# Forming the low halves of the attention weights on GpSimd instead of VectorE, in a two-block transformer kernel

## The chip, the cores and the metric

The kernel runs on one core of a Trainium2 chip. A core has several engines that run side by side, each through its own queue of instructions in a fixed order: TensorE (PE; its weight loads are listed as PEld), VectorE (DVE), ScalarE (ACT), GpSimd (POOL) and SyncE (SP), which here issues the transfers from memory. They wait for each other through semaphores. SBUF is the working memory that all of them reach, PSUM the one into which PE writes its products. The metric is the time of one execution on the device, in microseconds, lower is better; the number compared is the median of several runs.

## The reference

Two transformer blocks, one after the other, on 512 tokens of width 1024, all in float32. The first has a differential attention, a SwiGLU feed-forward part, a sliding-window attention with sinks and a second feed-forward part; the second block has convolution mixers, a convolution feed-forward part, a windowed attention over the tokens and 256 context rows, and a last feed-forward part. The three attentions are the places of this change. Cut to their weights:

```python
# first attention
q, k, v = jnp.split(h @ w_qkv, [DA_QK, 2 * DA_QK], axis=-1)      # 1024 x 3072
...
return o.reshape(B, S, DA_V) @ w_o                                # 1024 x 1024
# second attention
k, v = jnp.split(rms_norm(x, kv_norm) @ w_kv, 2, axis=-1)         # 1024 x 512
q = (h @ w_q).reshape(B, S, SW_KV_HEADS, SW_GROUP, HEAD_DIM)      # 1024 x 1024
...
return o.reshape(B, S, SW_HEADS * HEAD_DIM) @ w_o
# third attention
q, k, v = jnp.split(h @ w_qkv, [Q_W, Q_W + KV_W], axis=-1)        # 1024 x 1536
...
y = jnp.moveaxis(out, 0, 1).reshape(bsz, length, Q_W) @ w_o
```

## The kernel before, in words

Every float32 matrix that goes into a product is split in two halves of PE's float32r format: `hi` is the value rounded to float32r (a cast, by ACT or by DVE), and `lo` is what the rounding left, `src - hi` (a subtraction, by DVE). A product is then three matmuls, hi x hi, hi x lo and lo x hi, added up in PSUM (`mm3`).

Weights are loaded by `wload`: a transfer of 128 partitions x 1024 columns (512 KB; 768 columns for some) into one of two raw buffers, then `split` into one of three slots of a `hi` and a `lo` tile. A raw buffer is free for the next transfer when its subtraction is done, a slot when PE has read it for the last time. With `gain=` (the key, value and query weights of the second attention) another path is taken that multiplies by a norm's gain. The first two weights of the first attention are loaded with `urgent=0`, before everything else.

The three attentions are `diff_attn` and two calls of `gqa` (`cfg` 1 and 2). Each interleaves projections of the next heads with the softmax of the current ones (`weave`). In `gqa`, POOL copies one column for each head and block (`nc.gpsimd.tensor_copy(e[:, n:n+1], ns)`), the sink's logit, which ACT's exponential reads together with the scores. Between the attentions stand the feed-forward parts and the mixers, where POOL has 120 additions of 128x256 for a convolution.

The order of the instructions is not that of the code. `Rec` collects all operations with their dependences; `issue` orders them by a list schedule: `forward` starts on each engine the ready operation of highest priority, with each operation's duration from `cost`, and `backward` sets the priorities; the seven rounds of it serve the whole program. Casts are `flex`: `forward` may put them on ACT or on DVE, whichever is planned to be free. So every change of an engine or of a cost can reorder all engines' queues, and the order is fixed when the program is built. Line 390 of the profile is the place where an ordered operation is issued, so all rows carry that line, and rows are told apart by engine, operation, tiles and size: `arenaF` holds float32 tiles, `arenaR` float32r tiles, `arenaZ` either, `psum_t` is PSUM. A weight's low half is the row TENSOR_TENSOR arenaR<-arenaF,arenaR of 128x1024 or 128x768.

Of the kernel before, what the change touches and what calls it, by code (L numbers as in the profile page):

```python
# [9 lines left out]
F32 = mybir.dt.float32  # L10
# [4 lines left out]
ALU = mybir.AluOpType  # L15
# [183 lines left out]
class _Eng:  # L199
    def __init__(self, rec, name):  # L200
        self._r, self._n = rec, name
# [5 lines left out]
class Rec:  # L207
# [112 lines left out]
    def cost(self, eng, fn, a, k, outs, ins):  # L320
        o = outs[0]
        n = self.fsize(o)
        ps = any(x.tensor.name == self.pname for x in ins)
        if eng == "tensor":
            dt = (k.get("rhs") if fn == "matmul" else a[1]).dtype
            if fn == "transpose":
                return 59 if dt == F32R else 109
            if dt == F32:
                return max(n * 1.685, 214)
            if dt == F32R:  # L330
                return max(n * 0.4222, 107)
            return max(n * 0.4222, 29)
        if eng == "scalar":
            return n / 1.2 + (51 if ps else 93) + (93 if len(ins) > 1 else 0) + (93 if len(outs) > 1 else 0)
        if eng == "sync":
            b = 4
            for _, c in o.ap:
                b *= c
            return b
        if fn in ("tensor_tensor_reduce", "scalar_tensor_tensor") and isinstance(k["scalar"], bass.AP):  # L340
            return (n + 124) / 0.96
        if fn == "reduce_sum":
            n = self.fsize(ins[0])
        if eng == "gpsimd":
            return 2.1 * n + 148 if fn == "tensor_tensor" else 80 + n
        one = fn in ("tensor_copy", "tensor_scalar", "memset", "tensor_scalar_mul") and not ps
        return ((n / 2 if one and n > 64 else n) + 65) / 0.96

# [168 lines left out]
class Ker:  # L517
    def __init__(self, tc, a, es, start, stop):
        self.tc, self.a, self.start, self.stop = tc, a, start, stop
        real = tc.nc  # L520
        cp = es.enter_context(tc.tile_pool(name="arena", bufs=1))
        pp = es.enter_context(tc.tile_pool(name="banks", bufs=1, space=PSUM))
        self.psum = pp.tile([P, 8 * 512], F32, name="psum_t")[:]
        self.rec = self.nc = Rec(real, self.psum)
        self.bg = iter(())
        self.wslot = 0
        self.cls = {}
        self.size = {"R": R_SIZE, "F": F_SIZE, "Z": Z_SIZE}
        self.ar = {}
        for n, dt in (("R", F32R), ("F", F32)):  # L530
            self.ar[n] = cp.tile([P, self.size[n]], dt, name=f"arena{n}")[:]
            self.rec.rows[self.ar[n].tensor.name] = (n, self.size[n])
        self.zpool = None
        self.zmode = None
        self.nz = 0
        self.top = {"R": 0, "F": 0}
        self.flip = False
        self.psets = {}
        self.segment("R")
# [64 lines left out]
                              **{q: w for q, w in zip(names[1:], shape[1:])})  # L604
        return ap

    def phase(self, psets, keep=(), wslots=3):


        self.wslots = wslots  # L610
        self.wslot %= 3
        keep = dict(zip("RF", keep))
        if not keep:
            self.flip = not self.flip
        self.lo, self.hi = dict(self.top), {m: self.size[m] for m in "RF"}
        for m, w in keep.items():
            if self.flip:
                self.hi[m] -= w
            else:
                self.lo[m] += w  # L620
        self.zlo = 0
        self.cls = {k: v for k, v in self.cls.items() if k[0] not in ("ph", "z")}
        self.psets = {k: [v, 0] for k, v in psets.items()}
# [37 lines left out]
        o, w = _ROWS[name]  # L661
        return self.rowt[:, o:o + w] if o < NROW1 else self.rowd[:, o - NROW1:o - NROW1 + w]

    def split(self, src, hi, lo, scale=None):

        self.copy(hi, src)
        self.nc.vector.tensor_tensor(out=lo, in0=src, in1=hi.bitcast(F32), op=ALU.subtract)

    def rsqrt(self, v, n, y, ln=None):

# [36 lines left out]
    def wload(self, src, n=1024, gain=None, urgent=1000000, parts=1):  # L707

        nc = self.nc
        raw = self.t("wp", [1024], "wraw", bufs=2)[:, :n]  # L710
        j = self.wslot
        self.wslot = (j + 1) % self.wslots
        pool = "wp" if j < 3 else "ph"
        hi, lo = (self.t(pool, [1024], f"w{x}{j}", F32R)[:, :n] for x in ("hi", "lo"))
        rec = self.rec
        b, rec.bias = rec.bias, -urgent
        if gain is None:
            for x in range(parts):
                sl = slice(x * n // parts, (x + 1) * n // parts)
                self.dma(raw[:, sl], src[:, sl])  # L720
                self.split(raw[:, sl], hi[:, sl], lo[:, sl])
        else:
            self.dma(raw, src)
            k = n // len(gain)
            for j, g in enumerate(gain):
                sl = slice(j * k, (j + 1) * k)
                nc.scalar.activation(hi[:, sl], raw[:, sl], AF.Copy, scale=g)
                nc.vector.scalar_tensor_tensor(out=lo[:, sl], in0=raw[:, sl], scalar=g, in1=hi[:, sl].bitcast(F32),
                                               op0=ALU.mult, op1=ALU.subtract)
        rec.bias = b  # L730
        return hi, lo
# [621 lines left out]
    def diff_attn(self, X):  # L1353
        nc, a = self.nc, self.a
        if True:
            ph = None
            self.phase({"g": [0, 1], "r": [2], "s": [3, 4], "t": [5, 6], "o": [7], "f": [2, 3, 4, 7]})
            X.x = [None] * KT
            X.h = [None] * KT
            w0 = []  # L1360
# [32 lines left out]
            o, res, v = {}, {}, {}  # L1393
# [53 lines left out]
            for h in range(8):  # L1447
                fill = []
                if h < 7:
                    r = qks[h + 1][1]  # L1450
# [275 lines left out]
    def gqa(self, X, C, cfg):  # L1726
# [4 lines left out]
        if True:  # L1731
            ph = None
            if b2:
# [1 line left out]
                at = self.cls["ph", "t2l"][1] - 512  # L1735
                spare = {("ph", w): ["R", at + x, 1024, 1, 0] for w, x in (("whi3", 0), ("wlo3", 1024))}
            self.phase({"g": [0, 1], "s": [2, 3], "n": [4], "t": [5, 6], "o": [7]} if b2 else
                       {"g": [0, 1], "r": [2], "s": [3, 4], "t": [5, 6], "o": [7]})
            if b2:
                tab = (self.t("ph", [4, 1, 64], "axC"), self.t("ph", [4, 1, 64], "axS"), 1)  # L1740
                ax = a["axial"].rearrange("p (s a o d) -> p s a o d", s=2, a=4, o=1)
# [62 lines left out]
            o = {}  # L1804
# [25 lines left out]
            r, p = qs[0][1], qs[1][0]  # L1830
            for x in (r, r, p, r, r, p):
                next(x)
            for g in range(4):
                fill = []
                if g < 3:
                    r = qs[g + 1][1]
# [459 lines left out]
```

## Time and profile before

| | |
|---|---|
| runs, device time | 2524.76, 2527.75, 2531.60 us; median 2527.75 |
| the profiled execution | 2529.82 us, its span on the core 2528.0 us, mean granted PE clock 0.997 |
| busy in the span | PE 2493.7, PEld 2312.1, DVE 2198.9, ACT 1446.9, POOL 133.0 us |
| first attention | to about 252 us |
| second attention | about 603 to 800 us; its softmax part from 690 |
| third attention | about 1900 to 2145 us |

The span is what the profiler saw from the first to the last instruction. Busy times are unions of records; a matmul's end is modelled, so PE can be short of its peak where it is shown busy. Positions in the rows are us from the start of the span. Every duration used is of this one execution.

### The profile page before, as it was taken

How to read it: one execution, taken by the hardware profiler on the slowest of the kernel's cores; microseconds unless marked ns; L12 is line 12 of the kernel's file. 1: busy time of each engine (PE TensorE's matmuls, PEld its weight loads, DVE VectorE, ACT ScalarE, POOL GpSimd, SP SyncE). 2: the span in 40 equal slices, each digit the busy share in tenths (PEclk: the TensorE clock that was granted, in tenths of full speed). 3: DMA queues.
4: the chain of work that ended last, by engine and by line, in shares of the span. 5: the costliest groups of instructions: out<-in, count | busy, mean ns of one | idle time of the engine just before them, and what ended most of it. 6: DMA issues, size and time to landing. Idle time of an engine off the chain costs nothing.

```text
span 2528.0 us, 42483 instructions
## 1 busy us (share of the span) xinstructions
PE 2493.7 (99%) x16346; PEld 2312.1 (91%) x16346; DVE 2198.9 (87%) x4210; ACT 1446.9 (57%) x2795; POOL 133.0 (5%) x252
## 2 busy tenths in 40 slices
PE   8999999999999999999999999999999999999998
PEld 8998988888988989999889999999999988999897
DVE  8887999996699989888986998888887899998886
ACT  6877622223798545456664844434456798555464
POOL 0000000000010000003650000000000000000000
PEclk9999999999999999999999999999999999999999
DMA  4111566662213354432121121222221101323322
GB/s 146 62 55 65 188 204 221 211 214 89 76 37 123 125 185 144 168 131 84 51 76 59 43 76 59 75 67 76 68 70 56 43 26 51 109 84 100 115 75 89
DMA packets 73068, 252.52 MB, mean 100 GB/s; under 512 B 8480, under 2 KB 10656, under 8 KB 72608
## 3 DMA queue, kind: packets, MB, share of 16 engines
q1 hardware_dynamic: 72864, 249.80, 29.0%
q8 instruction: 128, 2.10, 0.3%
q14 instruction: 76, 0.62, 0.1%
HBM read 247.67 MB, written 2.10 MB: 99 GB/s over the span
## 4 chain that ended last, share of the span: by engine, by line
PE 92%; DVE 3%; POOL 2%; ACT 2%; issue 1%; DMA 0%; SPq 0%; DVEq 0%; POOLq 0%; ACTq 0%
PE psum_t L390 92%; POOL arenaZ L390 2%; DVE arenaF L390 2%; DVE arenaR L390 1%; ACT arenaR L390 1%; ACT arenaF L390 1%; DMA arenaF<-in_wqkv_dram 0%; SPq L390 0%; ACT L390 0%; ACT arenaZ L390 0%; ACT L388 0%; DVEq L2292 0%; POOLq L390 0%; ACT psum_t L390 0%; DVE psum_t L390 0%
## 5 line engine op out<-in xcount | busy, mean ns | idle before, releaser
L390 PE MATMUL psum_t<-arenaR 128*128 128x256 f32 (+3 forms) x13220 | 2156.4, 316 | 16.5 <-ACT arenaR L390 8.1
L390 PEld LDWEIGHTS psum_t<-arenaR 128*128 128x128 f32 (+1 forms) x13220 | 1917.4, 189 | 151.9 <-ACT arenaR L390 11.0
L390 ACT CAST arenaR<-arenaF 128x1024 fp32r<-128x1024 f32 (+5 forms) x622 | 537.8, 874 | 612.4 <-PE psum_t L390 397.4
L390 DVE TENSOR_TENSOR arenaR<-arenaF,arenaR 128x1024 fp32r<-128x1024 f32 (+5 forms) x586 | 599.7, 1033 | 73.0 <-ACT arenaR L390 64.6
L390 ACT ACTIVATE arenaF<-arenaF 128x256 f32<-128x256 f32 (+10 forms) x946 | 498.4, 552 | 171.7 <-DVE arenaF L390 138.5
L390 PE MATMUL psum_t<-arenaZ,arenaR 128*128 128x256 f32 (+3 forms) x2112 | 452.5, 326 | 1.4 <-ACT arenaZ L390 0.9
L390 DVE TENSOR_TENSOR arenaF<-arenaF 128x512 f32<-128x512 f32 (+7 forms) x715 | 404.4, 582 | 26.6 <-ACT arenaF L390 22.3
L390 PEld LDWEIGHTS psum_t<-arenaZ,arenaR 128*128 128x128 f32 x2112 | 335.2, 188 | 34.1 <-DVE arenaF L390 1.7
L390 DVE TENSOR_TENSOR arenaF<-psum_t,arenaF 128x256 f32<-128x256 f32 (+2 forms) x420 | 196.6, 482 | 80.8 <-PE psum_t L390 79.6
L390 DVE SCALAR_TENSOR_TENSOR arenaF<-arenaF 128x511 f32<-128x511 f32 (+9 forms) x555 | 244.0, 473 | 6.9 <-ACT arenaF L390 5.4
L390 DVE CUSTOM_DVE_ANT_0 arenaF<-arenaF 128x1024 f32<-128x1024 f32 x160 | 204.7, 1279 | 8.3 <-DMA arenaF<-in_wmod_dram 4.6
L390 DVE SCALAR_TENSOR_TENSOR arenaF<-psum_t,arenaF 128x256 f32<-128x256 f32 (+3 forms) x293 | 167.1, 595 | 35.5 <-PE psum_t L390 34.5
L390 ACT COPY arenaF<-psum_t 128x256 f32<-128x256 f32 (+2 forms) x285 | 106.7, 389 | 143.0 <-PE psum_t L390 133.3
L390 ACT CAST arenaR<-psum_t 128x512 fp32r<-128x512 f32 (+4 forms) x333 | 156.9, 480 | 31.3 <-PE psum_t L390 28.1
L390 POOL TENSOR_TENSOR arenaZ<-arenaZ,arenaF 128x256 f32<-128x256 f32 x120 | 103.1, 861 | 428.9 <-ACT arenaF L390 420.0
L390 PE MATMUL psum_t<-arenaF 128*128 128x128 f32 (+2 forms) x730 | 112.6, 268 | 7.4 <-DVE arenaF L390 3.2
L390 DVE CUSTOM_DVE_ANT_0 arenaF<-psum_t,arenaF 128x256 f32<-128x256 f32 (+3 forms) x208 | 103.6, 510 | 13.4 <-PE psum_t L390 11.5
L390 POOL COPY arenaF<-arenaF 128x1 f32<-128x1 f32 x128 | 29.7, 256 | 1565.6 <-issue 637.8
L390 DVE TENSOR_TENSOR arenaR<-psum_t,arenaR 128x512 fp32r<-128x512 f32 (+4 forms) x169 | 98.0, 589 | 14.8 <-ACT arenaR L390 13.3
L390 PEld LDWEIGHTS psum_t<-arenaF 128*128 128x128 f32 x730 | 89.3, 153 | 19.0 <-DVE arenaF L390 3.8
L390 ACT ACTIVATE arenaR<-arenaF 128x256 fp32r<-128x256 f32 (+1 forms) x152 | 72.1, 513 | 26.8 <-DVE arenaF L390 16.8
L390 DVE SCALAR_TENSOR_TENSOR psum_t<-arenaF,psum_t 128x512 f32<-128x512 f32 x120 | 81.8, 745 | 1.6 <-ACT psum_t L390 1.5
(53 smaller groups left out, 618.0 us busy)
## 6 DMA issues: line engine op xcount, KB each, us to landing
arenaF<-in_wmod_dram SPq DMA_DIRECT2D x96, 512.0 KB, 3.9
arenaF<-in_wgu_dram SPq DMA_DIRECT2D x88, 512.0 KB, 3.6
arenaF<-in_wup_dram SPq DMA_DIRECT2D x88, 512.0 KB, 3.2
arenaF<-in_wqkv_dram SPq DMA_DIRECT2D x35, 512.0 KB, 3.2
arenaF<-in_wdn_dram SPq DMA_DIRECT2D x30, 512.0 KB, 4.1
arenaF<-in_wd_dram SPq DMA_DIRECT2D x32, 448.0 KB, 3.7
arenaF<-in_wab_dram SPq DMA_DIRECT2D x20, 512.0 KB, 3.2
arenaF<-in_wd_dram SPq DMA_DIRECT2D x16, 512.0 KB, 3.3
```

Source lines behind the costliest of these rows:

```text
L390: getattr(getattr(self.nc, e), fn)(*a, **k)
```

## The change

`split` gets a switch that puts the subtraction on POOL, `wload` throws it in the phases that are opened with `lowpool=True` (the three attentions) unless the load has `urgent=0` or a gain, and `cost` gets another price for a POOL operation on two tensors of 512 columns or more. Sixty subtractions move: 32 in the first attention (8 of 768 columns), 8 in the second, 20 in the third.

```diff
-            return 2.1 * n + 148 if fn == "tensor_tensor" else 80 + n
+            return (2.1 * n + 148 if n < 512 else 3.36 * n) if fn == "tensor_tensor" else 80 + n
...
-    def phase(self, psets, keep=(), wslots=3):
+    def phase(self, psets, keep=(), wslots=3, lowpool=False):
...
         self.wslots = wslots
+        self.lowpool = lowpool
...
-    def split(self, src, hi, lo, scale=None):
+    def split(self, src, hi, lo, pool=False):
 
         self.copy(hi, src)
-        self.nc.vector.tensor_tensor(out=lo, in0=src, in1=hi.bitcast(F32), op=ALU.subtract)
+        eng = self.nc.gpsimd if pool else self.nc.vector
+        eng.tensor_tensor(out=lo, in0=src, in1=hi.bitcast(F32), op=ALU.subtract)
...
-                self.split(raw[:, sl], hi[:, sl], lo[:, sl])
+                self.split(raw[:, sl], hi[:, sl], lo[:, sl], self.lowpool and urgent)
...
-            self.phase({"g": [0, 1], "r": [2], "s": [3, 4], "t": [5, 6], "o": [7], "f": [2, 3, 4, 7]})
+            self.phase({"g": [0, 1], "r": [2], "s": [3, 4], "t": [5, 6], "o": [7], "f": [2, 3, 4, 7]}, lowpool=True)
...
-                       {"g": [0, 1], "r": [2], "s": [3, 4], "t": [5, 6], "o": [7]})
+                       {"g": [0, 1], "r": [2], "s": [3, 4], "t": [5, 6], "o": [7]}, lowpool=True)
```

Three places of the queues follow, as they stand in the two programs. POOL's queue from the mixers to the third attention, where the 128x1024 rows are the subtractions and the 128x1 rows the sink columns:

```order
 L390 TENSOR_TENSOR arenaZ_10453<-arenaZ_10453,arenaF 128x256 x120
-L390 COPY arenaF<-arenaF 128x1 x64
-L2292 UNCONDITIONAL_BRANCH
-L2292 ISA
+L390 TENSOR_TENSOR arenaR<-arenaF,arenaR 128x1024 x4
+L390 COPY arenaF<-arenaF 128x1 x12
+L390 TENSOR_TENSOR arenaR<-arenaF,arenaR 128x1024 x5
+L390 COPY arenaF<-arenaF 128x1 x3
```

The third attention's 64 copies stood together; now its 20 subtractions stand before and between them, the first four ahead of all copies.

DVE's queue about twenty rows into the program, at the start of the first attention, before the change. The 128x1024 row is a weight's low half; the other rows are sums of squares, the input's low halves and small table work:

```order
L390 TENSOR_TENSOR arenaR<-arenaF,arenaR 128x1024
L390 TENSOR_TENSOR arenaF<-arenaF 128x512
L390 SCALAR_TENSOR_TENSOR arenaF<-arenaF 128x128
L390 CAST arenaR<-arenaF 128x128
L390 TENSOR_SCALAR arenaF<-arenaF 128x128
L390 TENSOR_TENSOR arenaF<-arenaF 128x128 x2
L390 TENSOR_REDUCE arenaF<-arenaF 128x2
```

The same place in the changed program:

```order
L390 TENSOR_TENSOR arenaF<-arenaF 128x512
L390 SCALAR_TENSOR_TENSOR arenaF<-arenaF 128x128
L390 TENSOR_TENSOR arenaF<-arenaF 128x128
L390 TENSOR_SCALAR arenaF<-arenaF 128x128
L390 TENSOR_REDUCE arenaF<-arenaF 128x2
```

The low half is gone and the rows behind it have closed up; most of those that are left read two operands from SBUF.

PE's queue from the beginning of the program, before the change (128x256 are projections, the 128x128 rows from `arenaR` transposes of the first head's queries and keys):

```order
L390 MATMUL psum_t<-arenaR 128x256 x122
L390 MATMUL psum_t<-arenaF 128x1 x4
L390 MATMUL psum_t<-arenaR 128x256 x164
L390 MATMUL psum_t<-arenaR 128x128 x4
L390 MATMUL psum_t<-arenaR 128x256 x9
```

And in the changed program:

```order
L390 MATMUL psum_t<-arenaR 128x256 x115
L390 MATMUL psum_t<-arenaF 128x1 x4
L390 MATMUL psum_t<-arenaR 128x256 x123
L390 MATMUL psum_t<-arenaR 128x128 x4
L390 MATMUL psum_t<-arenaR 128x256 x19
```

The first transposes have moved ahead of 48 projections' matmuls.

## Rows read from the trace of the kernel before

**Rows 1.** The page, part 1: busy us, share of the span, instructions.

```profile
PE 2493.7 (99%) x16346; PEld 2312.1 (91%) x16346; DVE 2198.9 (87%) x4210; ACT 1446.9 (57%) x2795; POOL 133.0 (5%) x252
```

**Rows 2.** Busy us by stretch: length, engines (instructions), PE clock, DMA share, GB/s.

```profile
16.00:75.00 59.00, 58.96 (x495) 58.63 (x496) 52.15 (x145) 43.79 (x101) 0.00 (x0) 1.00 0.29 96
75.00:252.00 177.00, 174.54 (x1309) 165.01 (x1307) 149.95 (x416) 133.92 (x330) 0.00 (x0) 0.99 0.18 60
690.00:800.00 110.00, 105.24 (x713) 90.60 (x712) 103.05 (x286) 106.48 (x294) 10.57 (x48) 1.00 0.21 73
1900.00:1925.00 25.00, 21.20 (x157) 19.95 (x156) 21.74 (x56) 16.06 (x36) 0.00 (x0) 0.94 0.29 98
1925.00:2145.00 220.00, 216.09 (x1565) 200.33 (x1565) 192.02 (x466) 184.52 (x372) 13.98 (x64) 0.99 0.11 39
```

**Rows 3.** Groups on DVE, 16:252 (two), 690:800, 1900:2145: count | busy, mean ns | idle before.

```profile
L390 DVE TENSOR_TENSOR arenaR<-arenaF,arenaR 128x1024 fp32r<-128x1024 f32 x24 | 29.3, 1219 | 3.9 <-ACT arenaR L390 3.8
...
L390 DVE TENSOR_TENSOR arenaR<-arenaF,arenaR 128x768 fp32r<-128x768 f32 x8 | 7.6, 955 | 2.3 <-ACT arenaR L390 2.3
...
L390 DVE TENSOR_TENSOR arenaR<-arenaF,arenaR 128x1024 fp32r<-128x1024 f32 x8 | 9.7, 1215 | 0.3 <-ACT arenaR L390 0.3
...
L390 DVE TENSOR_TENSOR arenaR<-arenaF,arenaR 128x1024 fp32r<-128x1024 f32 x20 | 24.4, 1219 | 7.9 <-ACT arenaR L390 7.9
```

**Rows 4.** POOL: a group in 1194.8:1204.5, and the timeline at 685 (start, length).

```profile
L390 POOL TENSOR_TENSOR arenaZ<-arenaZ,arenaF 128x256 f32<-128x256 f32 x12 | 8.9, 739 | 0.9
...
685.32 0.18 POOL L390 COPY arenaF<-arenaF 128x1 f32<-128x1 f32 x1 [106.51 <-ACT arenaF L390]
```

**Rows 5.** Timelines of POOL and of DVE in the mixers, about 1190.4:1195.

```profile
1190.49 5.04 POOL L390 TENSOR_TENSOR arenaZ<-arenaZ,arenaF 128x256 f32<-128x256 f32 x4
...
1190.97 1.34 DVE L390 TENSOR_TENSOR arenaR<-arenaF,arenaR 128x1024 fp32r<-128x1024 f32 x1
1192.23 0.74 DVE L390 SCALAR_TENSOR_TENSOR psum_t<-arenaF,psum_t 128x512 f32<-128x512 f32 x1
1192.89 1.21 DVE L390 TENSOR_TENSOR arenaR<-arenaF,arenaR 128x1024 fp32r<-128x1024 f32 x1
```

**Rows 6.** Timeline of DVE in the first attention, five places.

```profile
19.10 1.22 DVE L390 TENSOR_TENSOR arenaR<-arenaF,arenaR 128x1024 fp32r<-128x1024 f32 x1
20.24 0.68 DVE L390 TENSOR_TENSOR arenaF<-arenaF 128x512 f32<-128x512 f32 x1
...
39.85 1.22 DVE L390 TENSOR_TENSOR arenaR<-arenaF,arenaR 128x1024 fp32r<-128x1024 f32 x1
...
42.51 0.69 DVE L390 TENSOR_TENSOR arenaR<-arenaF,arenaR 128x512 fp32r<-128x512 f32 x1
...
78.57 1.22 DVE L390 TENSOR_TENSOR arenaR<-arenaF,arenaR 128x1024 fp32r<-128x1024 f32 x1
79.71 0.75 DVE L390 SCALAR_TENSOR_TENSOR arenaF<-psum_t,arenaF 128x512 f32<-128x512 f32 x1
80.37 0.55 DVE L390 CUSTOM_DVE_ANT_0 arenaF<-psum_t,arenaF 128x384 f32<-128x384 f32 x1
...
80.84 0.42 DVE L390 TENSOR_TENSOR arenaF<-arenaF 128x256 f32<-128x256 f32 x1
...
251.04 1.20 DVE L390 TENSOR_TENSOR arenaR<-arenaF,arenaR 128x1024 fp32r<-128x1024 f32 x1
252.16 0.20 DVE L390 SCALAR_TENSOR_TENSOR arenaF<-arenaF 128x1 f32<-128x1 f32 x1
```

**Rows 7.** Timeline of DVE in the third attention, two places.

```profile
1914.44 1.22 DVE L390 TENSOR_TENSOR arenaR<-arenaF,arenaR 128x1024 fp32r<-128x1024 f32 x1
1915.57 0.49 DVE L390 TENSOR_TENSOR arenaF<-arenaF 128x2 f32<-128x2 f32 x2
...
2134.13 1.22 DVE L390 TENSOR_TENSOR arenaR<-arenaF,arenaR 128x1024 fp32r<-128x1024 f32 x1
2135.26 0.69 DVE L390 TENSOR_TENSOR arenaR<-psum_t,arenaR 128x512 fp32r<-128x512 f32 x1
```

More of the change, by code (lines that the diff above doesn't have):

```diff
@@ L526, in __init__ @@
         self.wslot = 0
+        self.lowpool = False
         self.cls = {}
```

## The prediction

> **What bounds the kernel now.** The page's first part comes first: TensorE (PE) is busy 2493.7 of 2528.0 us and VectorE (DVE) 2198.9 [rows 1]. A change that only takes load from DVE can therefore pay only where PE waits for DVE. So I cut the span by stage [rows 2]. 16:75 and 75:252 are the first attention (the first 16 us fill the pipeline), 690:800 is the softmax part of the second, 1900:1925 the beginning of the third and 1925:2145 its rest. The reader is to see how little PE idles there: 0.0, 2.5, 4.8, 3.8 and 3.9 us, 15 us in all, and that DVE is nearly full in three of these stretches (52.15 of 59, 103.05 of 110, 21.74 of 25). Outside them, but for their edges, the order of PE's instructions is the same in both programs, so I price these stretches alone.
>
> **What is removed and added.** Sixty subtractions leave DVE: 24 of 128x1024 and 8 of 128x768 in the first attention, 8 in the second, 20 in the third, at 1219 and 955 ns each [rows 3]. Records overlap a little: from the start of one to the start of the next row it is 1.14 us (19.10 to 20.24 in [rows 6]), and three quarters of it, 0.86, for the narrow ones. 52 x 1.14 + 8 x 0.86 = 66 us of DVE time are given back.
>
> The same sixty go to GpSimd (POOL), which in these stages did next to nothing. The trace shows its subtraction or addition of two SBUF operands only at 128x256: 739 ns when undisturbed; its smallest copy, one column, takes 0.18 us [rows 4]. From both: 0.18 + 0.56 x 1023/255 = 2.43 us for 1024 columns, if 0.18 is fixed cost; four times 739 = 2.96 us if nothing is fixed. I take the lower, since the one-column row shows that some of it is fixed, and keep 2.96 for the range.
>
> **What that does to DVE.** POOL and DVE exclude each other when both read two operands from SBUF. [Rows 5] show it both ways. Four POOL additions took 5.04 us in place of four times 0.74, because two of them met DVE's 128x1024 subtraction; and that subtraction, starting at 1190.97 while POOL was at work, took 1.34 us, not 1.22. The row between them, with one operand in PSUM, took its usual 0.74. So a POOL subtraction of 2.43 us stops DVE at the next row that reads two SBUF operands, until POOL is done.
>
> The Trainium skill has this as a rule (SBUF — State Buffer, "Who interferes with whom"): the port pair is an exclusive lock, and a DVE instruction with two SBUF inputs blocks against a GpSimd instruction that reads SBUF, the second to start waiting for the whole of the first. The trace agrees, with the rows just named. Without that rule the 66 us would simply be saved on DVE and the sum below would have no positive term for blocking.
>
> How long DVE is stopped I read at each of the sixty places: put POOL's 2.43 us (2.96) where the subtraction started, let DVE go on with the rows behind it, and count from the first row with two SBUF operands. [Rows 6] have the first and the last of the 32 of the first attention and one between. At 19.10 the next row is such a row: 2.43 lost. At 78.57 two rows with a PSUM operand come first (0.66 and 0.47): 1.30 lost. At 251.04: 2.43. Where DVE was idle anyway, idle time is not counted as lost. [Rows 7] have the third attention: at 1914.44 all is lost, at 2134.13 nothing, since that stage's rows read PSUM.
>
> **The sum, stretch by stretch** (blocked, less given back).
> 1. 16:75, nine subtractions: 19.3 (24.1) blocked, 10.3 given back, so DVE needs 9 (14) us more and would have 61 (66) us of work in 59 us [rows 2]: 2 to 7 us over. The new order makes it worse. PE's first small transposes now stand behind 115 + 123 matmuls, not 122 + 164: 48 x 0.119 us (58.96 us over 495 matmuls in [rows 2]) = 5.7 us sooner. What they wait for is DVE's subtraction at 42.51, behind five of the nine [rows 6], and that comes later. PE: +2 if other matmuls fill, 7 + 5.7 = +13 if none do; I take +6.
> 2. 75:252, 23 subtractions: 30.9 (40.8) blocked, 24.0 given back; DVE goes from 149.95 to 157 (167) of 177. It still fits, so PE sees only single late results: 0 to +6 (a third of the 17), I take +2.
> 3. 690:800, eight: 7.6 (9.8) blocked, 9.1 given back. PE's 4.8 us of waits shrink by up to 1.5 or grow by 1: I take -1.
> 4. 1900:1925, four: 9.2 (11.4) blocked, 4.6 given back; DVE goes from 21.74 to 26.4 (28.5) of 25. PE: +1.4 where the stretch's slack takes the rest, +6.8 where nothing does; I take +4.
> 5. 1925:2145, sixteen: 9.0 (13.2) blocked, 18.2 given back. DVE gains 5 to 9 us, and PE gets back at most the 3.9 it idled: I take -2.
>
> 6 + 2 - 1 + 4 - 2 = +9 us; ends -2 and +27. The profiled execution took 2529.82 us (span 2528.0), 2.1 above the median of the runs, 2527.75; so 2538.8 on its scale and about 2537 for the median.
>
> The Trainium skill (GPSIMD Engine Reference, "Elementwise — side-by-side cycle accounting") gives 4497 ns for 2048 columns. Half of it, 2.25 us, is my estimate from that page for 1024; no run here shows it, and with it each stop would be 0.18 shorter and the sum about +7.
>
> **What costs nothing, and its cover.** The low half itself is ready 1.2 to 1.7 us later. PE's weights are loaded ahead in three slots and the new order plans 3.4 us for the step, so other matmuls stand in between; without that cover it is 1.2 us at each of the nine loads of stretch 1, which its upper end holds. The raw buffers (two) are freed later by as much, and so SP's next transfer starts later: nine loads in 59 us leave 13 us for each use of a buffer, far more than transfer, cast and subtraction need together, except in stretch 4, where four follow in a row; its upper end holds that. Six more of the 128x1024 casts go to DVE in the new order (11, before 5): less than 1.22 us each, and off ScalarE by as much; I take nothing.
>
> **The rivals.**
> *Faster (0.18).* The stops fall into times when DVE would wait anyway, and the stages that read PSUM gain. For it: PE's 4.8 and 3.9 us in stretches 3 and 5 hang on a DVE and a ScalarE that are nearly full, and both lose load. Against: in 1 and 4 DVE has almost no idle time and every row reads SBUF twice. It decides where stretches 1 and 4 together cost PE under 1 us. Then -8.7 + 1 = -8: 2520.
> *No change (0.20).* PE has matmuls enough to fill each stop, as it did in 16:75 with a DVE at 88%. Terms 1 and 4 shrink to +2 and +1.4 and the rest cancels: 2529.
> *A queue on POOL (0.12).* In the second and third attention POOL also presets one column for each softmax (128 copies of 0.18 us), and in the new order 16 subtractions of the third stand between those copies. A copy behind one is 2.4 to 3 us late, and ScalarE's exponentials read that column. Against: the copies are issued early. If each of the 16 delays a chain by 1.5 us and PE fills half, +12 on top of the sum: 2549.
>
> **How the numbers follow.** The forecast, +9, has 0.50; its own range is 2526 to 2555. Under 0.3% (7.6 us), which is about what a measurement of this kernel can tell from no change, lie perhaps 0.12 of that, and all of the second rival: same 0.32. Slower: 0.38 + 0.12 = 0.50. Faster 0.18. Leaving out a tenth on each side of these cases gives 2519 to 2558.
>
> **What would show it.** POOL rows of 128x1024 at 2.4 to 3 us undisturbed. DVE rows with two SBUF operands stretched by up to that much in 16:75 and at the third attention's start, and rows with a PSUM operand unchanged. PE waits for DVE in 16:75, where there are none now. The second attention's waits a little smaller. The forecast is wrong if PE stays full to 75 us, if POOL's row is far from 2.43, or if ScalarE is seen waiting for POOL.

## The result, and the profile after

The changed kernel takes 2562.9 us (median of four runs, 2562.5 to 2564.7) against 2527.8 us before: slower, 1.0139 times, 95% interval 1.0122 to 1.0157. Forecast were 2537 us and a range up to 2558. The profiled execution took 2563.2 us (span 2561.4), 33.4 us more than that of before.

The page, part 1, and the two groups of the new operation on POOL (count | busy us, mean ns | idle before):

```profile
PE 2501.7 (98%) x16346; PEld 2316.7 (90%) x16346; DVE 2206.6 (86%) x4169; ACT 1438.0 (56%) x2776; POOL 274.1 (11%) x312
```

```profile
L390 POOL TENSOR_TENSOR arenaR<-arenaF,arenaR 128x1024 fp32r<-128x1024 f32 x52 | 128.8, 2479 | 890.2 <-ACT arenaR L390 789.9 <-PE psum_t L390 42.5 <-DVE arenaR L390 26.6
L390 POOL TENSOR_TENSOR arenaR<-arenaF,arenaR 128x768 fp32r<-128x768 f32 x8 | 15.5, 1944 | 39.0 <-ACT arenaR L390 37.3 <-PE psum_t L390 1.7
```

Against [rows 1] DVE is 7.7 us busier although sixty subtractions have left it: what they cost came back as longer rows, and as nineteen other rows that the new order gives to DVE (4169 instructions, where 4210 less sixty would be 4150). The price of the step on POOL, 2.48 us, is close to the forecast's 2.43.

To set stage against stage I matched the two traces by PE's work: the same count of matmuls from the same place on. The five stretches of [rows 2] are these in the profile after (length, then busy us and instructions of PE, PEld, DVE, ACT, POOL, PE's clock, DMA share, GB/s):

```profile
16.00:92.60 76.60, 63.46 (x495) 61.78 (x495) 62.28 (x154) 43.84 (x106) 23.82 (x9) 0.93 0.21 73
92.60:287.30 194.70, 179.32 (x1306) 166.28 (x1305) 155.79 (x393) 130.64 (x320) 52.00 (x23) 0.97 0.17 57
724.00:833.00 109.00, 105.20 (x707) 90.01 (x706) 101.58 (x283) 103.10 (x286) 31.37 (x57) 1.00 0.19 69
1935.40:1960.10 24.70, 20.81 (x157) 20.41 (x156) 22.22 (x51) 15.27 (x35) 7.84 (x3) 0.86 0.20 68
1960.10:2180.20 220.10, 213.71 (x1565) 198.51 (x1564) 186.32 (x460) 180.15 (x366) 52.40 (x81) 1.00 0.12 43
```

The loss is all in the first attention: the 495 matmuls that took 59.0 us take 76.6, the next 1300 or so 194.7 in place of 177.0. That is +17.6 and +17.7. The second attention's stretch is a microsecond shorter (with six matmuls fewer in it), the two of the third are as long as before. Of the 35.3 us, 26.0 are idle time of PE (13.1 + 15.4, before 0.0 + 2.5) and 9.3 are matmuls that take longer in sum (63.46 for 58.96, 179.32 for 174.54), at a granted clock of 0.93 and 0.97 in place of 1.00 and 0.99.

What PE waits for in the first attention, after (16:300) and before (16:265): us in total, times, longest.

```profile
PE psum_t L390 <- DVE arenaF L390: 16.5, 16, 3.1
PE psum_t L390 <- DVE arenaR L390: 10.9, 5, 5.3
PE psum_t L390 <- ACT arenaR L390: 1.7, 3, 0.7
```

```profile
PE psum_t L390 <- DVE arenaF L390: 2.7, 2, 2.3
PE psum_t L390 <- ACT arenaZ L390: 0.9, 1, 0.9
PE psum_t L390 <- DVE arenaR L390: 0.5, 1, 0.5
```

It waits for DVE, 21 times, never for POOL: the low halves are not late, DVE's own results are. The longest wait, in the timeline of DVE, POOL and PE (start, length, rows joined where the count is over 1, idle before <- releaser):

```profile
37.81 2.38 DVE L390 SCALAR_TENSOR_TENSOR arenaF<-arenaF 128x16 f32<-128x16 f32 x1
40.11 0.14 DVE L390 TENSOR_SCALAR arenaF<-arenaF 128x1 f32<-128x1 f32 x1
40.22 3.38 DVE L390 TENSOR_TENSOR arenaF<-arenaF 128x512 f32<-128x512 f32 x2
43.53 0.86 DVE L390 SCALAR_TENSOR_TENSOR arenaR<-psum_t,arenaF,arenaR 128x256 fp32r<-128x256 f32 x2
...
37.26 5.19 POOL L390 TENSOR_TENSOR arenaR<-arenaF,arenaR 128x1024 fp32r<-128x1024 f32 x2 [5.14 <-ACT arenaR L390]
...
37.36 1.79 PE L390 MATMUL psum_t<-arenaR 128*128 128x256 f32 x13 [1.24 <-DVE arenaF L390]
44.44 1.86 PE L390 MATMUL psum_t<-arenaR 128*128 128x256 f32 x7 [5.29 <-DVE arenaR L390]
```

Two POOL subtractions stand back to back from 37.26 to 42.45. A DVE row of 16 columns, 0.17 us elsewhere, takes 2.38; one of 512 columns, 0.69 elsewhere, is stopped by the second. The rows behind them make what PE needs at 39.15 and gets at 44.44. And then the clock pays as well (same columns as the stretches above):

```profile
39.00:45.00 6.00, 0.71 (x4) 0.56 (x3) 6.00 (x8) 0.00 (x0) 3.45 (x2) 0.75 0.47 171
45.00:50.00 5.00, 5.00 (x30) 5.00 (x29) 4.10 (x8) 0.62 (x1) 0.00 (x0) 0.62 0.03 8
50.00:55.00 5.00, 5.00 (x46) 5.00 (x45) 0.69 (x1) 4.01 (x10) 0.00 (x0) 1.00 0.00 0
```

PE stood still for 5.3 us, and the granted clock fell from 1.00 (2.4 GHz): its mean is 0.75 from 39 to 45 us and 0.62 in the next five, most of which is at 1.2 GHz. There 30 matmuls ran where 46 fit afterwards.

### The profile page after: what moved, and what is told of

It reads as the page before. It is cut to its first block, busy times and chain, and to the rows that moved or that the text cites. A ratio compares the mean times of both kernels' runs of the same rounds, so it can differ in the third digit from the quotient of the medians.

```text
span 2561.4 us, 42527 instructions
## 1 busy us (share of the span) xinstructions
PE 2501.7 (98%) x16346; PEld 2316.7 (90%) x16346; DVE 2206.6 (86%) x4169; ACT 1438.0 (56%) x2776; POOL 274.1 (11%) x312
## 4 chain that ended last, share of the span: by engine, by line
PE 85%; DVE 9%; POOL 2%; ACT 2%; issue 1%; DMA 0%; SPq 0%; DVEq 0%; POOLq 0%; ACTq 0%
PE psum_t L390 85%; DVE arenaF L390 7%; POOL arenaZ L390 2%; DVE arenaR L390 2%; ACT arenaR L390 1%; ACT arenaF L390 1%; DMA arenaF<-in_xT_dram 0%; DVE arenaZ L390 0%; SPq L390 0%; ACT arenaZ L390 0%; ACT L390 0%; POOLq L390 0%; DVEq L2295 0%; ACT psum_t L390 0%; DVE psum_t L390 0%
## 5 line engine op out<-in xcount | busy, mean ns | idle before, releaser
L390 PE MATMUL psum_t<-arenaR 128*128 128x256 f32 (+2 forms) x13220 | 2166.1, 317 | 36.8 <-DVE arenaR L390 16.3
L390 PEld LDWEIGHTS psum_t<-arenaR 128*128 128x128 f32 x13220 | 1921.0, 189 | 173.3 <-ACT arenaR L390 17.3
L390 ACT CAST arenaR<-arenaF 128x1024 fp32r<-128x1024 f32 (+5 forms) x616 | 531.0, 874 | 637.6 <-PE psum_t L390 405.0
L390 ACT ACTIVATE arenaF<-arenaF 128x512 f32<-128x512 f32 (+10 forms) x939 | 497.6, 554 | 195.4 <-DVE arenaF L390 162.6
L390 DVE TENSOR_TENSOR arenaR<-arenaF,arenaR 128x1024 fp32r<-128x1024 f32 (+5 forms) x526 | 532.3, 1024 | 60.2 <-ACT arenaR L390 52.7
L390 DVE TENSOR_TENSOR arenaF<-arenaF 128x512 f32<-128x512 f32 (+7 forms) x715 | 427.8, 616 | 29.4 <-ACT arenaF L390 22.9
L390 DVE SCALAR_TENSOR_TENSOR arenaF<-arenaF 128x511 f32<-128x511 f32 (+9 forms) x555 | 270.6, 523 | 8.0 <-ACT arenaF L390 5.6
L390 POOL TENSOR_TENSOR arenaR<-arenaF,arenaR 128x1024 fp32r<-128x1024 f32 (+1 forms) x60 | 144.3, 2407 | 929.2 <-ACT arenaR L390 827.2
L390 ACT CAST arenaR<-psum_t 128x512 fp32r<-128x512 f32 (+5 forms) x328 | 154.5, 479 | 28.8 <-PE psum_t L390 25.5
L390 DVE CUSTOM_DVE_ANT_0 arenaF<-psum_t,arenaF 128x256 f32<-128x256 f32 (+3 forms) x208 | 103.4, 512 | 25.1 <-PE psum_t L390 23.6
L390 DVE TENSOR_TENSOR arenaR<-psum_t,arenaR 128x512 fp32r<-128x512 f32 (+4 forms) x169 | 98.9, 591 | 12.3 <-ACT arenaR L390 11.1
```

What stands on the lines that cost most here:

```text
L390: getattr(getattr(self.nc, e), fn)(*a, **k)
```

## The experiments

Two numbers recur for each kernel, both from its profiled execution. "Stops" are the time by which DVE's rows were stretched beside POOL's work on low halves: for each such row its duration less the lower quartile of all rows of the same operation and shape in that trace, summed from 0 to 310 us. "Loss" is how much later than before PE reaches the work that it had reached at 300 us, that is, behind the first attention. The changed kernel has 41.5 us of stops and 34.2 of loss there. A loss of a microsecond or two can't be told from chance: the last kernel below has the order and the engines of before in its whole first attention and stands 1.8 us late by this measure, all of it from before 16 us.

**Order and engine apart.** The first edit leaves the new order and gives the subtractions back to DVE:

```diff
+            if e == "gpsimd" and fn == "tensor_tensor" and self.fsize(k["out"]) >= 512:
+                e = "vector"
             getattr(getattr(self.nc, e), fn)(*a, **k)
```

> The order of every engine as in the changed kernel, but the sixty subtractions run on VectorE at the places that the order gives them. Theory of stops (GpSimd's subtractions hold VectorE's SBUF rows for up to 2.4 us, and TensorE waits for those rows): the stops are gone, 2528 to 2538 us, a few above the kernel before because 66 us of work come back to a VectorE that was planned without them. Theory of order (the new order, made with 3.44 us for a subtraction and a VectorE that runs beside it, brings TensorE's operands late whoever subtracts): 2555 us or more. Theory of late weights (low halves and raw buffers free later): 2528 to 2535, as a VectorE subtraction is short.

2555.6 us, 1.0115 (1.0100 to 1.0130); no stops, loss 15.0. Read then as the order's own cost, which a later run overturned.

The second plans as before (the subtraction is recorded for DVE) and issues it on POOL:

```diff
+            if i in self.swap:
+                e = "gpsimd"
             getattr(getattr(self.nc, e), fn)(*a, **k)
```

> The order of every engine as in the kernel before, but the sixty subtractions run on GpSimd. Theory of stops: 2550 to 2575 us, as in the changed kernel, since GpSimd holds VectorE for as long. Theory of order: 2525 to 2533. Theory of late weights: above 2545, with TensorE seen waiting for GpSimd, as this order plans the subtraction as if it took 1.14 us.

2555.3 us, 1.0113 (1.0098 to 1.0128); stops 47.0, loss 22.2. So the stops cost without any new order. PE waits for POOL 1.4 us in the first attention; late low halves explain little of the 22.2.

The third keeps the changed kernel's order and copies in place of subtracting. The expectation says that its waits are those of the changed kernel. That is not quite so: a copy reads the raw weights alone and does not wait for the cast that makes the high half. The second copy ends 0.95 us behind that cast (median of the first attention), the subtraction of the changed kernel 2.5.

```diff
+            if e == "gpsimd" and fn == "tensor_tensor" and self.fsize(k["out"]) >= 512:
+                for _ in range(2):
+                    self.nc.gpsimd.tensor_copy(out=k["out"], in_=k["in0"])
+                continue
```

> The changed kernel, but in place of each of the sixty subtractions GpSimd copies the raw weights twice into the low half (one operand from SBUF; the output is wrong, the low half is not the rest of the weights). Order and waits are those of the changed kernel. Theory of stops, where only a GpSimd row with two SBUF operands holds VectorE: 2528 to 2540 us. Theory of stops, where any GpSimd row that reads SBUF does: near 2560, if the two copies together last about as long as the subtraction (2.48 us). Theory of order: near 2560 either way. Late weights: near 2560 if the copies last as long.

2540.9 us, 1.0053 (1.0038 to 1.0068), loss 14.9. I took the copies for harmless, which with the loss of 15.0 of the first kernel made 15 us of "order" and 22 of "stops". The timeline of POOL and DVE shows the mistake:

```profile
15.07 2.99 POOL L392 CAST arenaR<-arenaF 128x1024 fp32r<-128x1024 f32 x2 [14.62 <-DMA arenaF<-in_par_dram]
...
15.63 1.52 DVE L394 SCALAR_TENSOR_TENSOR arenaR<-arenaF,arenaR 128x512 fp32r<-128x512 f32 x1
17.08 1.00 DVE L394 CAST arenaF<-arenaF 128x4 f32<-128x4 int32 x1
17.99 0.21 DVE L394 CAST arenaR<-arenaF 128x128 fp32r<-128x128 f32 x1
18.13 0.74 DVE L394 SCALAR_TENSOR_TENSOR arenaR<-arenaF,arenaR 128x512 fp32r<-128x512 f32 x1
```

A copy with one operand stops DVE as well, 0.8 us at a time (1.52 for 0.74); between the two copies one row gets through. This kernel has 21.3 us of stops.

The fourth takes `lowpool=True` out of the first attention's `phase` call alone.

> Only the 28 subtractions of the second and third attention go to GpSimd; the first attention is as in the kernel before. All theories: the loss of the changed kernel lies in its first 290 us, so this stands within 0.2% of the kernel before: 2524 to 2530 us by the matching of TensorE's rows (-0.5 us in the second attention, -1.5 in the third). Above 2535 would mean that the first attention's loss hides a loss of the later two.

2530.3 us, 1.0013 (1.0003 to 1.0022), just above the 2524 to 2530 that were expected. The first attention makes nearly the whole difference.

**The planner's part.** The price of the step on POOL, then a plan that knows the stops:

```diff
-            return (2.1 * n + 148 if n < 512 else 3.36 * n) if fn == "tensor_tensor" else 80 + n
+            return (2.1 * n + 148 if n < 512 else 2.2 * n + 180) if fn == "tensor_tensor" else 80 + n
```

> The changed kernel, with the planner's price for the 1024-column subtraction on GpSimd set from 3.44 us to the 2.43 us that the trace shows. Found so far: in the first attention the order alone costs 15 us (order of after with harmless copies on GpSimd), the stops alone 22 us. Theory A (the order costs because it was made with a price that is 1 us too high): the 15 us go, 2541 to 2550 us. Theory B (the order costs because its planner doesn't know the stops, or because any new order is worse than this one): 2555 to 2570 us.

2550.9 us, 1.0098 (1.0083 to 1.0113); stops 33.5, loss 22.9.

```diff
+            if e == "vector" and t < hold and self.port(ops[i]):
+                heapq.heappush(pend[e], (hold, i))
+                continue
             c = ops[i][5]
+            if e == "gpsimd" and c > 1600:
+                hold = t + c
```

> As the kernel with the price of 2.43 us, and in the plan a VectorE row without an operand in PSUM (reductions apart) can't start while GpSimd subtracts. Theory that the 22 us of stops are rows that TensorE waits for, which a plan could put elsewhere: 2535 to 2550 us. Theory that there is no room in VectorE's chain of the first attention, wherever the stops are put: 2555 us or more.

2541.6 us, 1.0057 (1.0042 to 1.0072); stops 17.8, loss 12.3. Against the kernel with the right price alone, a plan that gives DVE rows that are not held takes away nearly half of the stops, and the loss falls with them; it still does not reach the kernel before.

How much any new plan moves the time, with nothing on POOL: a factor on the price of the sixty subtractions on DVE, 1.06 and 0.94.

```diff
+        self.rec.mult = 1.06 if pool else 1.0
         self.nc.vector.tensor_tensor(out=lo, in0=src, in1=hi.bitcast(F32), op=ALU.subtract)
```

> The kernel before (all subtractions on VectorE), but the planner's price of the sixty subtractions is 6% higher, 1.20 us in place of 1.13; nothing else differs than the order that comes out. Theory of the redrawn order (the order of before is one of many and a lucky one, any new one costs): 2532 to 2545 us. Theory that the new order of the change is bad of itself (it takes the 66 us of VectorE time as free): 2524 to 2530 us.

> The same with a price 6% lower, 1.07 us. Theory of the redrawn order: 2532 to 2545 us, with the loss at other places than at a price 6% higher. Theory that the change's order is bad of itself: 2524 to 2530 us.

2533.1 us, 1.0024 (1.0015 to 1.0034), loss 4.4; and 2531.1 us, 1.0015 (1.0006 to 1.0024), loss 2.1. Drawing the order anew costs 2 to 4 us in the first attention (of which 2 may be chance); it is not the 34.

**Copies in other orders, and pieces.** The copies of above, in the order of the price of 2.43, in that of before, and in that which knows the stops:

> The order made with the price of 2.43 us, and two one-operand copies on GpSimd in place of each subtraction, which don't hold VectorE (the output is wrong: the low half is not the rest of the weights). What is left against the kernel before is the order's own cost at this price. Theory that the 15 us of the first order came from its price of 3.44 us: 2525 to 2532 us. Theory that any new order of this kind costs as much: 2537 to 2543.

2537.3 us, 1.0045 (1.0030 to 1.0060); stops 21.8, loss 11.6.

> The order of the kernel before, with two copies on GpSimd in place of each of the sixty subtractions (the output is wrong in the same way). Neither a new order nor stops are left, only 66 us less work on VectorE and low halves that come 1.2 us later. It measures what the time given back on VectorE is worth. If VectorE's time matters in these stages: 2515 to 2524 us. If TensorE's own work bounds them, as the idle time of 15 us says at most: 2522 to 2530. If the later low halves matter: above 2530, with TensorE waiting for GpSimd.

2533.5 us, 1.0027 (1.0016 to 1.0038); stops 25.1, loss 3.7.

> The order whose plan knows the stops, with two copies on GpSimd in place of each subtraction (the output is wrong in the same way). Beside the 2541.6 us of that order with subtractions it tells how much of the 15 us that are left is the order and how much is stops (17.9 us of VectorE rows stretched in its first attention). If the order: 2535 to 2541 us. If the stops: 2526 to 2534.

2539.3 us, 1.0051 (1.0035 to 1.0068); stops 15.6, loss 11.2. All three expectations took the copies for harmless. With their stops counted, the difference between copies and subtractions goes with the difference in stops (21.8 and 33.5 us against a loss of 11.6 and 22.9 in one order, 15.6 and 17.8 against 11.2 and 12.3 in the other). That nothing else sets them apart is not shown by two pairs, since the copies' low halves also come sooner.

The order of before again, with the subtraction on POOL cut in four, later in eight:

```diff
+                n4 = self.fsize(k["out"]) // 4
+                for x in range(4):
+                    sl = slice(x * n4, (x + 1) * n4)
+                    self.nc.gpsimd.tensor_tensor(out=k["out"][:, sl], in0=k["in0"][:, sl], in1=k["in1"][:, sl], op=k["op"])
+                continue
```

> The order of the kernel before, the sixty subtractions on GpSimd, each in four pieces of a quarter of the columns (0.74 us each for 256, as the trace of before shows for that size). A VectorE row is stopped for one piece, not for all four, but GpSimd's total grows from 2.47 to about 3 us. Theory that the length of a single stop costs (TensorE waits for the row that is stopped): 2532 to 2545 us, below the 2555 of the undivided one. Theory that the sum of the stops costs: 2555 us or more, and TensorE waits for GpSimd more than before.

2536.6 us, 1.0043 (1.0028 to 1.0058); stops 24.7, the longest 0.57, loss 6.4 (undivided: 47.0, 2.22 and 22.2), in a profiled execution that is 3.7 us above the median. The low half of this kernel is finished later than the undivided one, 3.4 us behind its cast in place of 2.5 (medians of the first attention), and yet most of the loss is gone: in this order it came from the stops and not from late low halves.

> The order of the kernel before, each subtraction on GpSimd in eight pieces. Theory of the sum of the stops: four pieces stretched VectorE's rows by 24.7 us in the first attention (47.0 undivided) and cost 6.4 us there; eight give perhaps 15 us of stops and 0 to 4 us lost, 2526 to 2533 in all. Theory of late low halves (GpSimd needs over 3.4 us for each): 2537 us or more, with TensorE waiting for GpSimd.

2544.1 us, 1.0069 (1.0054 to 1.0084); stops 17.2, loss 9.6: worse than four. Now the low halves are late. PE's waits from 16 to 300 us begin with POOL:

```profile
PE psum_t L399 <- POOL arenaR L397: 3.8, 8, 0.8
PE psum_t L399 <- DVE arenaF L399: 3.0, 1, 3.0
```

POOL's time for the first attention's low halves grows from 74.3 us undivided to 105.9 and 137.3. Most of the growth is the pieces themselves, about 90 and 113 us at their medians (0.74 us for 256 columns, 0.46 for 128); the rest is POOL waiting in its turn.

**No hold at all.** POOL writes zeros, which reads nothing, and subtracts one column, which still waits for the cast; the rest of the low half is left out. This is done in the order of before, in that of the change, and in one made with the first nine subtractions left on DVE (`pool and self.nlow > 9`):

```diff
+                self.nc.gpsimd.memset(k["out"].bitcast(F32), 0.0)
+                cut = {x: v[:, 0:1] if isinstance(v, bass.AP) else v for x, v in k.items()}
+                self.nc.gpsimd.tensor_tensor(**cut)
+                continue
```

> The order of the kernel before; in place of each of the sixty subtractions GpSimd fills the low half with zeros (reads nothing) and subtracts one column, so that the waits stay and almost no row of VectorE is held (the output is wrong, the low half is zero but for a column). If TensorE's loss goes nearly one to one with the stops once the time given back is used up, no stops should give back what there is: 2518 to 2525 us. If VectorE's 66 us are worth nothing: 2525 to 2530, and the 2533.5 of the copies was their 25 us of stops.

2523.2 us, 0.9987 (0.9978 to 0.9997); stops 0.4, loss -2.2.

> The order of the changed kernel, zeros and one column in place of each subtraction (the output is wrong in the same way). Theory that the order costs by itself: 2535 to 2542 us, the 15 us in the first attention that the copies and the subtractions on VectorE showed. Theory that the copies' stops (21 us) and, in the other kernel, VectorE's unplanned 66 us did it: 2525 to 2531.

2517.8 us, 0.9965 (0.9952 to 0.9978); stops 0.7, loss -0.2. 17 us below the theory of the order, which falls, and 7 below the other: when nothing holds DVE the changed order is 9.5 us faster than the kernel before, and 5.4 faster than the order of before without holds. The matched stretches of this kernel, and PE's waits from 16 to 300 us:

```profile
16.00:74.30 58.30, 58.02 (x490) 57.56 (x489) 46.36 (x153) 43.87 (x106) 10.73 (x17) 1.00 0.27 95
74.30:253.00 178.70, 175.28 (x1307) 165.93 (x1306) 130.67 (x393) 130.10 (x320) 26.17 (x46) 0.98 0.19 63
1899.40:1918.90 19.50, 18.70 (x156) 18.30 (x155) 17.45 (x52) 15.54 (x35) 4.90 (x7) 1.00 0.28 95
1918.90:2135.20 216.30, 213.60 (x1565) 198.59 (x1564) 180.40 (x459) 179.48 (x365) 28.25 (x97) 1.00 0.13 43
```

```profile
PE psum_t L395 <- DVE arenaF L395: 2.8, 3, 1.5
PE psum_t L395 <- ACT arenaR L395: 1.4, 2, 0.7
PE psum_t L395 <- DVE arenaR L395: 0.3, 1, 0.3
```

The same order on every engine as in the changed kernel, and PE's 27.4 us of waits for DVE are 3.1. The gain is in the third attention: 25.0 us of [rows 2] become 19.5 and 220.0 become 216.3.

> As the kernel before this one, but the first nine subtractions of the first attention stay on VectorE and are planned there; the order is made anew for that. If the order's cost sits where the small sums and transposes of the first 60 us are pulled forward: 2530 to 2535 us, with 0 to 2 us lost by 57 us. If it sits anywhere: 2535 to 2542.

2513.3 us, 0.9947 (0.9932 to 0.9961), faster than either theory had it; loss -3.7. At the work of 75 us it stands 0.2 us ahead of the kernel before this one: there was no cost in the first 60 us to be saved.

In these kernels the step on POOL was also shorter, 1.2 us. With the zeros written twice it is 2.1, but a fill need not wait for the cast and mostly runs ahead of it. POOL in the kernel with two fills:

```profile
46.21 1.96 POOL L392 MEMSET arenaR<- 128x1024 f32 x2
51.89 0.19 POOL L394 TENSOR_TENSOR arenaR<-arenaF,arenaR 128x1 fp32r<-128x1 f32 x1 [3.72 <-issue]
```

> The order of the changed kernel; GpSimd fills the low half with zeros twice and subtracts one column, 2.1 us in place of 1.2 with one fill and of 2.43 with the subtraction; almost nothing holds VectorE (the output is wrong, the low half is zero but for a column). If stops are the cause: as with one fill, 2516 to 2521 us. If low halves and raw buffers that come a microsecond later are: 2528 us or more, like the two copies (2540.9), whose step is as long.

2520.8 us, 0.9970 (0.9958 to 0.9982); stops 1.7, loss 0.6. This tests less than was meant. From the end of a cast to the end of its low half it is 0.3 us with one fill and 0.9 with two (medians of the first attention), but 2.5 in the changed kernel: 0.6 us later costs next to nothing (0.6 for -0.2), and the other 1.6 are not tested by it. Late low halves and raw buffers are ruled out by the waits of the changed kernel instead. Only PE reads a low half, and it never waits for POOL in the first attention; a raw buffer that is free late would show as a cast waiting for its transfer, and up to 300 us neither ScalarE nor DVE waits there for a weight. DVE waits for no transfer at all, and of ScalarE's waits these alone are for a transfer or for POOL (the transfers are the kernel's input, not a weight):

```profile
ACT L390 <- DMA arenaF<-in_xT_dram: 3.7, 1, 3.7
ACT arenaR L390 <- POOL arenaR L390: 2.1, 1, 2.1
ACT arenaR L390 <- DMA arenaF<-in_xT_dram: 0.9, 1, 0.9
```

With the four pieces above, which come later still and cost less, what is left is the stops.

**A version from all this.** Only the third attention's twenty subtractions on POOL (`lowpool=b2` in `gqa`, none in `diff_attn`), in four pieces:

> Only the twenty subtractions of the third attention on GpSimd, each in four pieces, in an order made with 3.44 us for them. In that stage the changed kernel without any hold gained 9.5 us, with whole subtractions (11.5 us of stops) 1.1, with two copies (7.1 us of stops) 4.0. Four pieces gave 7.4 us of stops there: a gain of 3 to 4 us, 2522 to 2525 us, 0.1 to 0.2% below the kernel before. If a divided subtraction is too late for TensorE in that order: 2527 us or more.

2524.5 us, 0.9988 (0.9979 to 0.9997), 2.9 us below the kernel before, inside the expectation. Its two stretches of the third attention:

```profile
1902.50:1924.80 22.30, 19.01 (x157) 18.41 (x156) 20.50 (x48) 14.53 (x32) 10.12 (x12) 1.00 0.18 64
1924.80:2143.70 218.90, 213.93 (x1565) 198.53 (x1564) 184.23 (x463) 181.17 (x367) 60.94 (x133) 1.00 0.13 44
```

2.7 and 1.1 us shorter than in [rows 2], of the 5.5 and 3.7 that are there without stops. It is the only version with the whole computation that stands below the kernel before, by a tenth of a per cent.

## Why the forecast was wrong

The kernels with the order of before and with that of the change side by side, first attention only (stops, loss, us):

```
on POOL                  order of before     order of the change
nothing but zeros          0.4    -2.2          0.7    -0.2
zeros twice                  -                  1.7    +0.6
two copies                25.1    +3.7         21.3   +14.9
four pieces               24.7    +6.4            -
eight pieces              17.2    +9.6            -
the whole subtraction     47.0   +22.2         41.5   +34.2
(on DVE)                   0       0            0     +15.0
```

In the order of the change 40.8 us of stops (41.5 less 0.7) cost PE 34.4: 0.84 us for each. In the order of before it is 24.4 for 46.6, 0.52. The price is not constant: the shorter stops of the copies cost 0.73 (15.1 for 20.6) and 0.24 (5.9 for 24.7), again more in the order of the change. Both columns start near zero, and the stops move them (in the last row 34 us of DVE work that the order had not planned, 0.44 for each; with eight pieces also the late low halves).

**Where the forecast was right.** POOL's price (2.43; measured 2.48, 2.35 to 2.40 undisturbed). The mechanism: rows with a PSUM operand go on beside POOL, rows with two SBUF operands stop, PE waits for DVE in 16:75 where it had not. The total of the stops was even too high: 50.2 us forecast for the first attention, 41.5 measured; 7.6 and 4.8 in the second; 18.2 and 11.5 in the third. Nothing came of the rival on POOL's queue: in the attention phases ScalarE waits once, 2.1 us, behind a low half's step, and never for the one-column copies.

**The step that failed: how stops become PE's loss.** The working took for each stretch "blocked, less given back" and let PE pay only what did not fit into DVE's idle time. Term 2 (75:252) had 31 us of stops less 24 given back and 20 us of idle time to spare, so +2; it measured +17.7. Term 1 had +6 with an upper end of 13; it measured +17.6. Neither subtraction is allowed:
- DVE's idle time there is not spare. It is time in which DVE itself waits for PE and ScalarE, as I read it inside chains that PE needs next. In the kernel with zeros and the same order DVE is busy only 130.7 of 178.7 us in the second stretch, 48 us idle; 27.0 us of stops there still make it 16.0 us longer (194.7). In the first stretch 14.5 us of stops cost 17.7, the fall of the clock with them (76.6, against 58.3 for 490 of the 495 matmuls). How late a row is counts, not how full its engine is.
- What is given back had been spent. The planner knew that DVE was free and moved rows and PE's early sums forward into that time; a stop then hits a plan without slack. That would be why the same stop costs 0.84 in the new order and 0.52 in the old one, whose plan still holds the time for the subtraction. This reading of the two slopes is argued; what speaks for it is the kernel with the new order and DVE subtracting, which loses 15 us without any stop.
- The 5.7 us for transposes that stand 48 matmuls sooner were no cost of their own: without stops that order does 490 of the 495 matmuls in 58.3 us.

**The other terms.** Term 3, -1: the row has -1.0, six matmuls of it by the cut; right within what can be read. Term 4, +4: measured -0.3. Term 5, -2: +0.1. Both of the third attention have more in them than I saw: without stops they gain 5.5 and 3.7 us, and the stops (11.5 us) eat that up. "Costs nothing" for late low halves and raw buffers held, up to four pieces.

Of the three signs named as proof against the forecast (PE full to 75 us, another price, ScalarE waiting for POOL) the first two did not appear and the third came to the one wait of 2.1 us; it failed at a fourth. The clock is part of it and had no term: about 9 of the 35 us are matmuls that ran longer, at a lower granted clock, behind the waits.

Open is which of DVE's idle stretches could take a stop for nothing: the plan that knew the stops still lost 12 us with 18 us of them.

## What to carry to other kernels

Do not net a stop on an engine against time given back on it, nor against its idle share: ask for the row that is stopped, who waits for it, and whether the plan has already spent the time. A stand-in in an experiment needs its own look at the trace before it counts as harmless: two copies passed for "no stop" in four kernels, and the zeros, which turned the conclusion round, took away a wait for the cast along with the stop. Where an operation must share a port, a few pieces can shorten the other engine's waiting until the operation itself comes late: here four pieces halved it (47.0 to 24.7 us) and were better than one, and eight were worse than four.

## What the runs showed of the hardware

- A GpSimd row with one SBUF operand holds DVE like one with two: 1.15 us of copy stretched DVE's rows by up to 0.89. Writing zeros (0.95 us for 1024 columns) held next to nothing, 0.4 to 0.7 us in 32 fills (0.5 of the 0.7 is one DVE cast of 128x1024 that took 1.20 us). The Trainium skill has both (SBUF — State Buffer, "Who interferes with whom"): a DVE instruction with two SBUF inputs contends with a GpSimd instruction that reads SBUF, not with one that only writes it. The trace agrees; I had cited the rule and yet took the copies for free.
- Held are also DVE rows with a single SBUF operand, if they are casts or TENSOR_SCALAR, down to four columns (timelines of DVE, then POOL, in the profile after):

```profile
16.72 2.39 DVE L390 CAST arenaF<-arenaF 128x4 f32<-128x4 int32 x1
...
16.30 2.79 POOL L390 TENSOR_TENSOR arenaR<-arenaF,arenaR 128x1024 fp32r<-128x1024 f32 x1 [15.86 <-DMA arenaF<-in_rows_dram]
...
28.83 0.90 DVE L390 SCALAR_TENSOR_TENSOR arenaF<-arenaF 128x128 f32<-128x128 f32 x4
29.63 2.57 DVE L390 TENSOR_SCALAR arenaF<-arenaF 128x128 f32<-128x128 f32 x2
...
28.35 3.77 POOL L390 TENSOR_TENSOR arenaR<-arenaF,arenaR 128x1024 fp32r<-128x1024 f32 x1 [3.74 <-ACT arenaR L390]
```

  The Trainium skill says in the same section (SBUF — State Buffer, "Who interferes with whom") that casts and TENSOR_SCALAR can enter a mode that takes the shared port pair. The trace agrees in that these rows are held; which mode they ran in it does not show. TENSOR_REDUCE (median 0.684 us beside POOL and away from it) and RECIPROCAL (0.156 and 0.156) are not held.
- It goes both ways: POOL's step at 28.35 took 3.77 us in place of 2.40, while DVE's rows above went on at their usual length until 29.8.
